# A row-half local operand, early work on the fourth quarter, and a doubled-step tail of the second scan chain in a one-core S5 / attention network

## The chip, the cores and the metric

The kernel runs on one core of a Trainium2 chip. The metric is the device time of one launch in microseconds (us), as the median of the runs given; one further execution was taken by the hardware profiler, and all rows below are from it. Engines are called as in the profile: PE (TensorE matmuls), PEld (TensorE weight loads), DVE (VectorE), ACT (ScalarE), POOL (GpSimd), SP (the DMA queue).

## What is computed

Two layers on one sequence of 256 tokens of width 2048. Layer 0 is an S5 state-space mixer, layer 1 a dilated windowed attention, each followed by a SwiGLU network. The change lies in the mixer alone:

```python
def s5_mixer(u, ...):                       # u: RMS-normed input, 128 groups of 16 channels
    lb  = exp((a_re + i a_im) * dt)         # 128 x 64 complex poles
    bb  = (lb - 1) / a * b                  # input map,  16 channels -> 64 states
    st[t] = lb * st[t-1] + bb @ u[t]        # a scan over the 256 tokens
    y[t]  = Re(c @ st[t]) + d * u[t]        # output map, 64 states -> 16 channels
    val, gate = split(gelu(y) @ w_glu)
    return val * sigmoid(gate)
```

## The kernel before

**Blocks of four tokens.** The 256 tokens are 64 blocks of four, so the scan has 63 steps by the fourth power of the poles. A block's output has two parts: `y_local`, from the four tokens of the block through a small dense operator `mt`, and `y_state`, from the state at the block's beginning through `fds`. The 128 groups are handled as four quarters (`qr` 0 to 3) of 32 groups; quarters 0 and 1 share the first scan chain (`sts[0]`), 2 and 3 the second (`sts[1]`). All helper calls of this function go through `InOrder`, so their instructions have line 59 in the profile, and stand on each engine in the order in which the code emits them.

**Order of the mixer.** Tables of powers and taps (DVE); `inject`: products that put each block's input into the states (PE, copied out by ACT); `build_m` for the four quarters (lines 458 to 478): the operator `mt`, then six small DMAs each that spread its bands; the scan (`scan`, lines 480 to 487: three DVE operations a step, one product by the table `fsc` and two additions, each needing the one before). `steps(n, sa, sb)` interleaves the two chains operation by operation. The first chain has a lead of 16 steps (`LEAD`), so when it is done (63 steps), 16 steps of the second remain; these are emitted in pieces between other DVE work (lines 650 to 670). While the scan runs, PE does `y_local` of quarters 0, 1, 2 and `y_state` for the first 32 blocks (`y_state(qr, yl[qr], range(8), 0, 32)`), and after the first chain's end `y_state` for blocks 32 to 63, `gelu` (ACT), `turn` (transposes on PE, high halves by ACT), `low` (low halves by DVE) and `feed` (the first block of the `w_glu` product: three matmuls of 512 columns for each part).

**`build_m` before.** Two groups' products stand side by side in a matmul with 128 rows and 64 columns. So that the two halves of the rows don't mix, `m_operand` (lines 450 to 456) writes a copy `cb` of `cp` with zeros in the other half, by ACT with a mask as scale: four ACT operations a quarter, queued on ACT behind the copies of the quarter before. Then 2 matmuls with the identity (256 columns, the skip term), 16 with `cb`, and two copies by ACT.

**PSUM.** `ps_ms` and `ps_tr` have two buffers each, `ps_mm` four. During the scan `ps_mm` holds its tables: `tbp` and `tbq` hold `fsc` and the scan's products `prs` until the second chain is done. Quarter 3's `y_local` is put into `ps_mm`, hence behind that chain (lines 679 and 680).

```python
        high(2, 0)
        feed(1, 1)
        rest(2, 0)
        y_state(2, yl[2], range(8), 32, 64)
        ...
        yl[3] = y_local(3, self.ps_mm, "mm")
        y_state(3, yl[3])
        turns(2)
```

From about 155 us on the program is a stream of weight chunks (1 MB each) with 512-column matmuls; nothing of the change touches it.

Of the kernel before, what the change touches and what calls it, by code (L numbers as in the profile page):

```python
# [20 lines left out]
P = 128  # L21
# [8 lines left out]
GI = 16  # L30
NS = 64
# [15 lines left out]

NW = 14
LEAD = 16


class InOrder:
# [9 lines left out]
class Net:  # L62
# [141 lines left out]
    def s5_glu(self):  # L204
        tc, nc, io = self.tc, self.nc, self.io
        late = tc.alloc_tile_pool(name="s5late", bufs=1)
        early = tc.alloc_tile_pool(name="s5early", bufs=1, side="right")
        V = nc.vector
        T, A, G, W = (InOrder(tc, e) for e in (nc.tensor, nc.scalar, nc.gpsimd, nc.vector))
# [35 lines left out]
        def tt(out, i, j, o, eng=None):  # L245
            (eng or V).tensor_tensor(out=out, in0=i, in1=j, op=o)
# [84 lines left out]
        pf = [form("pf1", lam)]  # L331
# [115 lines left out]
            for k in range(2):  # L447
                pair(cp[:, k, mo:mo + 16], cf[:, k, :, mo:mo + 16], ct[:, :, mo:mo + 16])

        def m_operand(qr, j4):  # L450
            m0 = 16 * qr + 8 * j4
            cb = early.tile([P, 2, 4, 2, 32], FP32, name="cb", tag="cb", bufs=2)
            src = cp[:, :, m0:m0 + 8].rearrange("p r (j x) o -> p r j (x o)", x=2)
            for y in range(2):
                A.activation(out=cb[:, :, :, y], in_=src, func=AF.Copy, scale=masks[:, y:y + 1])
            return cb

        def build_m(qr):
            cbs = [m_operand(qr, j4) for j4 in range(2)]
            ps = self.ps_ms.tile([P, 8, 2, 2, GI], FP32, name="ms")  # L460
            for xx in range(2):
                T.matmul(ps[:, :, :, xx], lhsT=self.ident,
                         rhs=dsm[:, 16 * qr:16 * qr + 16].rearrange("p (j y) o -> p j y o", y=2),
                         start=(xx == 0), stop=False, skip_group_check=True)
            for j in range(8):
                for ri in range(2):
                    T.matmul(ps[:, j], lhsT=gps[qr][:, ri, 2 * j:2 * j + 2].rearrange("p x s i -> p (x s i)"),
                             rhs=cbs[j // 4][:, ri, j % 4].rearrange("p y c -> p (y c)"),
                             start=False, stop=(ri == 1), skip_group_check=True)
            mo = 16 * qr  # L470
            for xx in range(2):
                r = slice(64 * xx, 64 * xx + 64)
                A.copy(out=mt[r, 3, mo:mo + 16].rearrange("p (j y) o -> p j y o", y=2), in_=ps[r, :, :, xx])
            for t in range(3):
                n = 16 * (t + 1)
                for xx in range(2):
                    nc.sync.dma_start(out=mt[64 * xx:64 * xx + n, t, mo:mo + 16],
                                      in_=mt[64 * xx + 64 - n:64 * xx + 64, 3, mo:mo + 16])

        def scan(h):  # L480
            st = sts[h]
            f, pr = fsc[h], prs[h]
            for c in range(63):
                hh, v = st[:, c], st[:, c + 1]
                yield lambda: tt(pr, f, hh.unsqueeze(1).broadcast_to([P, 2, 2, 32]), ALU.mult, W)
                yield lambda: tt(v, v, pr[:, :, 0], ALU.add, W)
                yield lambda: tt(v, v, pr[:, :, 1], ALU.add, W)

        def run(*its):
# [160 lines left out]
        for half in range(2):  # L650
            steps(3, sb)
            rest(0, half)
        steps(2, sb)
        pts = [turn(0, j4) for j4 in range(2)]
        y_state(1, yl[1], range(4, 8), 32, 64)
# [27 lines left out]
        feed(2, 0)  # L683
# [333 lines left out]
```

## Time and profile before

| quantity | us |
|---|---|
| median of 3 runs (2430.07 to 2431.36) | 2430.44 |
| the profiled execution's own time | 2428.69 |
| its span, first to last instruction | 2426.9 |
| PE busy in it | 2392.5 |
| DVE busy | 1323.8 |
| ACT busy | 1081.4 |

The profiled execution is 1.75 us below the median of the other runs; its span is 1.79 us below its own time. PE is busy for 99% of the span, but the profile counts a matmul that waits inside the engine as busy, and small fp32 matmuls are recorded as two matmuls and two weight loads each. A shape such as 64*128 in a row is rows*columns of the loaded weights; the shape behind it is what streams through.

### The profile page before, as it was taken

How to read it: one execution, taken by the hardware profiler on the slowest of the kernel's cores; microseconds unless marked ns; L12 is line 12 of the kernel's file. 1: busy time of each engine (PE TensorE's matmuls, PEld its weight loads, DVE VectorE, ACT ScalarE, POOL GpSimd, SP SyncE). 2: the span in 40 equal slices, each digit the busy share in tenths (PEclk: the TensorE clock that was granted, in tenths of full speed). 3: DMA queues.
4: the chain of work that ended last, by engine and by line, in shares of the span. 5: the costliest groups of instructions: out<-in, count | busy, mean ns of one | idle time of the engine just before them, and what ended most of it. 6: DMA issues, size and time to landing. Idle time of an engine off the chain costs nothing.

```text
span 2426.9 us, 29373 instructions
## 1 busy us (share of the span) xinstructions
PE 2392.5 (99%) x11856; PEld 1936.8 (80%) x11856; DVE 1323.8 (55%) x1974; ACT 1081.4 (45%) x1367; POOL 113.5 (5%) x113
## 2 busy tenths in 40 slices
PE   6899999999999999999999999999999999999999
PEld 5788888888888888888888888788888888888887
DVE  8955454454444454565446676765454444454454
ACT  7344444444334444554445555554444433344433
POOL 4800000000000000000000000100000000000000
PEclk9899999999999999999999999999999999999999
DMA  2345555555555555555554444445555555555554
GB/s 85 96 163 185 181 189 180 185 191 176 189 191 187 179 188 182 182 194 181 184 184 170 156 156 142 156 154 185 182 188 179 185 191 187 184 184 188 179 197 148
DMA packets 63033, 423.58 MB, mean 175 GB/s; under 512 B 8112, under 2 KB 9520, under 8 KB 12336
## 3 DMA queue, kind: packets, MB, share of 16 engines
q1 hardware_dynamic: 61744, 419.60, 50.7%
q8 instruction: 93, 1.52, 0.3%
q10 hardware_dynamic: 1152, 2.10, 0.2%
q14 instruction: 44, 0.36, 0.0%
HBM read 418.79 MB, written 2.10 MB: 173 GB/s over the span
## 4 chain that ended last, share of the span: by engine, by line
PE 97%; DVE 2%; ACT 1%; issue 0%; DMA 0%; POOL 0%; SPq 0%; DVEq 0%; POOLq 0%
PE mm L122 30%; PE mm L124 30%; PE mm L123 30%; PE ms L59 2%; PE tr L59 1%; PE ms L857 1%; PE tr L743 1%; PE mm L59 1%; PE tr L808 1%; DVE mm L59 0%; PE tr L857 0%; PE tr L185 0%; DVE gp L59 0%; DVE gpb L59 0%; PE ms L887 0%
## 5 line engine op out<-in xcount | busy, mean ns | idle before, releaser
L104 DVE TENSOR_TENSOR wlo<-raw,whi 128x1024 fp32r<-128x1024 f32 x776 | 948.5, 1224 | 1003.6 <-ACT whi L103 1002.1
L103 ACT CAST whi<-raw 128x1024 fp32r<-128x1024 f32 x776 | 813.0, 1048 | 1161.9 <-PE mm L124 1142.2
L122 PE MATMUL mm<-whi,actt 128*128 128x512 f32 x3104 | 1235.8, 398 | 1.4 <-ACT whi L103 1.4
L124 PE MATMUL mm<-whi,actt 128*128 128x512 f32 x3104 | 1229.6, 396 | 0.0
L123 PE MATMUL mm<-wlo,actt 128*128 128x512 f32 x3104 | 1229.3, 396 | 0.0
L124 PEld LDWEIGHTS mm<-whi,actt 128*128 128x128 f32 x3104 | 583.1, 188 | 139.2
L122 PEld LDWEIGHTS mm<-whi,actt 128*128 128x128 f32 x3104 | 583.1, 188 | 138.3 <-ACT whi L103 2.1
L123 PEld LDWEIGHTS mm<-wlo,actt 128*128 128x128 f32 x3104 | 583.2, 188 | 136.9 <-DVE wlo L104 0.4
L795 POOL TENSOR_TENSOR sc<-ssq,mhalf 128x8 f32<-128x8 f32 x16 | 32.1, 2005 | 475.0 <-DVE ssq L793 475.0
L174 POOL TENSOR_TENSOR r<-m,mhalf 128x1 f32<-128x1 f32 x6 | 3.2, 552 | 1053.1 <-DVE m L173 848.9
L59 DVE TENSOR_TENSOR actr<-actr,mm 128x64 f32<-128x64 f32 x252 | 46.7, 215 | 2.0
L729 ACT ACTIVATE sg<-mm,r 128x512 f32<-128x512 f32 x44 | 30.1, 690 | 21.3 <-PE mm L124 21.0
L59 DVE TENSOR_TENSOR mm<-mm,actr 128x128 f32<-128x128 f32 x126 | 37.0, 294 | 0.9
L866 ACT ACTIVATE s<-s,mx 128x384 f32<-128x384 f32 (+1 forms) x32 | 24.8, 774 | 25.1 <-DVE mx L864 25.1
L59 POOL TENSOR_TENSOR fpr<-pf,cp 128x512 f32<-128x512 f32 x32 | 34.9, 1092 | 0.0
L733 DVE SCALAR_TENSOR_TENSOR sg<-mm,r,sg 128x512 f32<-128x512 f32 x44 | 30.9, 742 | 0.0
L59 ACT COPY actr<-ms 128x252 f32<-128x252 f32 (+1 forms) x40 | 19.9, 580 | 22.5 <-PE ms L59 21.4
L791 ACT ACTIVATE sq<-mm 128x512 f32<-128x512 f32 x32 | 19.0, 594 | 23.5 <-PE mm L124 23.5
L871 DVE SCALAR_TENSOR_TENSOR p<-s,z,p 128x128 f32<-128x128 f32 (+1 forms) x64 | 26.3, 411 | 3.8 <-ACT p L869 3.6
L747 DVE TENSOR_TENSOR actt<-tr,actt 128x512 fp32r<-128x512 f32 x44 | 28.2, 681 | 0.0
L746 ACT CAST actt<-tr 128x512 fp32r<-128x512 f32 x44 | 23.7, 590 | 10.1 <-PE tr L743 10.1
L743 PEld LDWEIGHTS tr<-ident,sg 128*128 128x128 f32 x176 | 19.4, 140 | 9.2 <-DVE sg L733 9.2
(180 smaller groups left out, 946.8 us busy)
## 6 DMA issues: line engine op xcount, KB each, us to landing
raw<-w_gu SPq DMA_DIRECT2D x176, 1024.0 KB, 4.8
raw<-w_down SPq DMA_DIRECT2D x88, 1024.0 KB, 4.8
raw<-w_q SPq DMA_DIRECT2D x48, 1024.0 KB, 4.8
raw<-w_glu SPq DMA_DIRECT2D x32, 1024.0 KB, 4.8
raw<-w_kv SPq DMA_DIRECT2D x32, 1024.0 KB, 4.7
raw<-w_o SPq DMA_DIRECT2D x16, 1024.0 KB, 4.7
actr<-x_c SPq DMA_DIRECT2D x2, 1024.0 KB, 6.4
xr<-x_t SPq DMA_DIRECT2D x8, 256.0 KB, 5.8
```

Source lines behind the costliest of these rows:

```text
L59: return lambda *a, **k: self.tc.keep_in_program_order(call(*a, **k))
L103: (scalar or self.nc.scalar).copy(out=hi, in_=r)
L104: (vector or self.nc.vector).tensor_tensor(out=lo, in0=r, in1=hi.bitcast(FP32), op=ALU.subtract)
L122: matmul(ps[th], lhsT=a[:, 0, ts], rhs=hi, start=(k == 0), stop=False)
L123: matmul(ps[th], lhsT=a[:, 0, ts], rhs=lo, start=False, stop=False)
L124: matmul(ps[th], lhsT=a[:, 1, ts], rhs=hi, start=False, stop=(k == n - 1))
L729: nc.scalar.activation(out=s, in_=ps[th], func=AF.Silu, scale=rs[th])
L733: nc.vector.scalar_tensor_tensor(out=sg[th], in0=ps[th], scalar=rs[th], in1=sg[th], op0=ALU.mult, op1=ALU.mult)
L743: nc.tensor.transpose(out=pt[:, k, th * P:(th + 1) * P], in_=sg[th][:, c:c + P], identity=self.ident)
L747: nc.vector.tensor_tensor(out=ht[:, k0:k0 + 2, 1], in0=pt, in1=ht[:, k0:k0 + 2, 0].bitcast(FP32), op=ALU.subtract)
L795: nc.gpsimd.tensor_tensor(out=sc, in0=ssq, in1=self.mhalf.rearrange("p (a b) -> p a b", a=2), op=ALU.pow)
L871: nc.vector.scalar_tensor_tensor(out=pr, in0=sc[:, g], scalar=z, in1=pr, op0=ALU.mult, op1=ALU.add)
```

## The change

Three edits in the mixer, all before about 155 us.

**1. Row-half local operand.** `m_operand`, its masks and `cb` go. `build_m` now takes two PSUM tiles a quarter, one for each half of the rows: quarters 0 and 2 from `ps_ms`, 1 and 3 from `ps_tr`. The identity term is 4 matmuls of 128 columns instead of 2 of 256; the products are 32 matmuls of 64 rows and 32 columns, alternating between the two halves, instead of 16 of 128 rows and 64 columns; ACT copies four times 64x128 instead of twice 64x256.

**2. Second chain's tail.** `sb` ends after 47 steps (`LAST`). The squared table `f8` (eight tokens) is made by six DVE operations (`square`), interleaved with the first chain's solo steps. `tail`: four more single steps, interleaved with 18 operations (`lead_in`) that add each odd injection, times the table, to the next one for the last 12 blocks; then six units (`doubles`), each giving two blocks from one state: one product by `f8`, one by `fsc`, four additions.

**3. Quarter 3 ahead.** `y_local(3)` goes to `ps_ms` and, with `y_state(3)` for blocks 0 to 31, stands directly behind `feed(1, 1)`; blocks 32 to 63 follow after `gelu(yl[2])`. `turn` of quarters 2 and 3 takes `ps_mm` instead of `ps_ms`. The pieces of `sb` between `rest(0, 0)` and `rest(0, 1)` are four steps' worth of operations instead of three.

```diff
-        def m_operand(qr, j4):
-            ...
-                A.activation(out=cb[:, :, :, y], in_=src, func=AF.Copy, scale=masks[:, y:y + 1])
         def build_m(qr):
-            cbs = [m_operand(qr, j4) for j4 in range(2)]
-            ps = self.ps_ms.tile([P, 8, 2, 2, GI], FP32, name="ms")
-            ...
+            pool, nm = ((self.ps_ms, "ms"), (self.ps_tr, "tr"))[qr % 2]
+            ps = [pool.tile([P, 8, 2, GI], FP32, name=nm) for _ in range(2)]
             ...
             for j in range(8):
                 for ri in range(2):
-                    T.matmul(ps[:, j], lhsT=gps[qr][:, ri, 2 * j:2 * j + 2]...,
-                             rhs=cbs[j // 4][:, ri, j % 4]...)
+                    for y in range(2):
+                        r = slice(64 * y, 64 * y + 64)
+                        T.matmul(ps[y][:, j], lhsT=gps[qr][r, ri, 2 * j:2 * j + 2]...,
+                                 rhs=cp[r, ri, mo + 2 * j:mo + 2 * j + 2]...)
@@
-            for c in range(63):
+            for c in range(63 if h == 0 else LAST):
@@
+        def lead_in(c0):
+            for c in range(c0, 63, 4):
+                for k in range(2):
+                    yield lambda: tt(w4[k], f, st[:, c + 1 + 2 * k]..., ALU.mult, W)
+                for r in range(2):
+                    for k in range(2):
+                        v = st[:, c + 2 + 2 * k]
+                        yield lambda: tt(v, v, w4[k][:, :, r], ALU.add, W)
+        def doubles(c0):
+            for c in range(c0, 63, 2):
+                hh, v, w = (st[:, c + k] for k in range(3))
+                yield lambda: tt(pr8, f8, b, ALU.mult, W)
+                yield lambda: tt(prs[1], f, b, ALU.mult, W)
+                for r in range(2):
+                    yield lambda: tt(w, w, pr8[:, :, r], ALU.add, W)
+                    yield lambda: tt(v, v, prs[1][:, :, r], ALU.add, W)
@@
-        steps(LEAD - 6, sa)
+        run(itertools.islice(sa, 3 * (LEAD - 6)), square())
@@
+        sb = tail()
@@ def turn
-            pt = self.ps_ms.tile([P, 4, 2, NS], FP32, name="ms")
+            pt = (self.ps_ms.tile(..., name="ms") if qr < 2 else self.ps_mm.tile(..., name="mm"))
@@
         feed(1, 1)
+        yl[3] = y_local(3, self.ps_ms, "ms")
+        y_state(3, yl[3], range(8), 0, 32)
         rest(2, 0)
         y_state(2, yl[2], range(8), 32, 64)
         ...
         gms[2] = gelu(yl[2])
-        yl[3] = y_local(3, self.ps_mm, "mm")
-        y_state(3, yl[3])
+        y_state(3, yl[3], range(8), 32, 64)
         turns(2)
```

How the instructions now stand, at the places that matter. On PE, the four quarters of `build_m` (`cb` masked operand, `cp` plain operand, `gp_228` to `gp_231` the weights of quarters 0 to 3, `dsm` the skip term), before:

```order
L59 MATMUL ms<-dsm,ident 128x16x16 x2
L59 MATMUL ms<-cb,gp_228 128x64 x16
L59 MATMUL ms<-dsm,ident 128x16x16 x2
L59 MATMUL ms<-cb,gp_229 128x64 x16
L59 MATMUL ms<-dsm,ident 128x16x16 x2
L59 MATMUL ms<-cb,gp_230 128x64 x16
L59 MATMUL ms<-dsm,ident 128x16x16 x2
L59 MATMUL ms<-cb,gp_231 128x64 x16
```

and now:

```order
L60 MATMUL ms<-dsm,ident 128x8x16 x4
L60 MATMUL ms<-cp,gp_228 128x32 x32
L60 MATMUL tr<-dsm,ident 128x8x16 x4
L60 MATMUL tr<-cp,gp_229 128x32 x32
L60 MATMUL ms<-dsm,ident 128x8x16 x4
L60 MATMUL ms<-cp,gp_230 128x32 x32
L60 MATMUL tr<-dsm,ident 128x8x16 x4
L60 MATMUL tr<-cp,gp_231 128x32 x32
```

Twice as many matmuls of half the rows and half the columns, and the odd quarters write the other pool. On PE, from the last `feed` of the second chunk to the transposes of quarter 2 (`mm<-actr`, `ms<-actr`: `y_local` 64x64 and `y_state`, 32x64 for half of the blocks), before:

```order
L59 MATMUL tr<-whi,actt 128x512
L59 MATMUL mm<-actr 32x64 x64
L59 MATMUL mm<-actr 64x64 x96
L59 MATMUL ms<-ident,gm 128x128 x8
L59 MATMUL tr<-whi,actt 128x512
```

and now:

```order
L60 MATMUL tr<-whi,actt 128x512
L60 MATMUL ms<-actr 64x64 x32
L60 MATMUL ms<-actr 32x64 x64
L60 MATMUL mm<-actr 32x64 x64
L60 MATMUL ms<-actr 32x64 x64
L60 MATMUL mm<-ident,gm 128x128 x8
L60 MATMUL tr<-whi,actt 128x512
```

`y_local(3)` and half of `y_state(3)` moved ahead of quarter 2's second half, and `y_state(3)` is 128 matmuls of 32 instead of 64 of 64. On SP, the last six band copies (`actr<-actr`, quarter 3) and the first weight chunks, before:

```order
L477 DMA actr<-actr 48x256 x2
L96 DMA raw<-w_glu 128x2048
L477 DMA actr<-actr 16x256 x2
L477 DMA actr<-actr 32x256 x2
L477 DMA actr<-actr 48x256 x2
L96 DMA raw<-w_glu 128x2048 x2
L699 DMA xr<-x_t 128x512 x8
```

and now:

```order
L475 DMA actr<-actr 48x256 x2
L475 DMA actr<-actr 16x256 x2
L475 DMA actr<-actr 32x256 x2
L475 DMA actr<-actr 48x256 x2
L97 DMA raw<-w_glu 128x2048 x3
L752 DMA xr<-x_t 128x512 x8
```

The first chunk of `w_glu` stands behind those six copies instead of ahead of them.

## Rows read from the trace of the kernel before

**Rows 1.** The page: span; busy time, share and instructions of each engine; the shares of the chain that ended last by engine.

```profile
span 2426.9 us, 29373 instructions
...
PE 2392.5 (99%) x11856; PEld 1936.8 (80%) x11856; DVE 1323.8 (55%) x1974; ACT 1081.4 (45%) x1367; POOL 113.5 (5%) x113
...
PE 97%; DVE 2%; ACT 1%; issue 0%; DMA 0%; POOL 0%; SPq 0%; DVEq 0%; POOLq 0%
```

**Rows 2.** The chain that ended last, in order of time, 50 to 158 us: start, length, engine and tile ("issue": the engine waits for nothing that the profile shows).

```profile
61.42 0.69 ACT cb L59 x2
62.16 3.80 PE ms L59 x32
...
73.29 13.86 PE ms L59 x68
...
87.99 3.47 PE ms L59 x60
...
97.22 3.24 issue
...
103.23 5.78 PE mm L59 x172
...
110.91 0.83 issue
...
129.46 9.47 PE mm L59 x302
```

**Rows 3.** Busy time by stretch: from:to, length, busy us of PE, PEld, DVE, ACT, POOL, then the granted clock of TensorE (1.00 is 2.4 GHz, 0.50 is 1.2 GHz), DMA share and GB/s.

```profile
62.00:74.00 12.00, 10.11 (x78) 9.21 (x79) 12.00 (x79) 5.74 (x15) 11.53 (x14) 1.00 0.08 21
74.00:76.00 2.00, 2.00 (x19) 2.00 (x18) 2.00 (x14) 0.04 (x1) 1.92 (x3) 0.91 0.22 61
76.00:92.00 16.00, 15.56 (x127) 14.39 (x127) 16.00 (x106) 4.66 (x10) 15.29 (x19) 0.50 0.28 91
...
100.00:106.00 6.00, 5.54 (x145) 5.37 (x145) 5.86 (x37) 0.00 (x0) 5.76 (x7) 0.50 0.03 5
```

**Rows 4.** PE in order of time, the four quarters of `build_m`: start, length, instructions; in brackets the idle time before and what ended it.

```profile
60.47 1.10 PE L59 MATMUL ms<-dsm,ident 128*128 128x256 f32 x4
62.16 3.79 PE L59 MATMUL ms<-cb,gp 128*128 128x64 f32 x32 [0.59 <-ACT cb L59]
65.78 1.08 PE L59 MATMUL ms<-dsm,ident 128*128 128x256 f32 x4
67.73 3.79 PE L59 MATMUL ms<-cb,gp 128*128 128x64 f32 x32 [0.87 <-ACT cb L59]
...
73.29 4.97 PE L59 MATMUL ms<-cb,gp 128*128 128x64 f32 x32 [0.86 <-ACT cb L59]
...
80.05 7.09 PE L59 MATMUL ms<-cb,gp 128*128 128x64 f32 x32
```

**Rows 5.** PE in order of time, 14 to 53 us: the transposes of the second half's input, whose weights have 64 rows and 128 columns.

```profile
38.33 1.21 PE L59 MATMUL tr<-ident,actr 64*128 64x64 f32 x16
39.37 1.16 PE L59 MATMUL ms<-ident,actr 64*128 64x64 f32 x16
```

**Rows 6.** Weight loads by shape, 37 to 40 us and 50 to 60 us: count, busy us, mean ns of one, idle before.

```profile
L59 PEld LDWEIGHTS tr<-ident,actr 64*128 64x128 f32 x16 | 1.1, 139 | 0.2 <-issue 0.2
...
L59 PEld LDWEIGHTS tr<-ident,gp 128*128 128x128 f32 x16 | 1.7, 140 | 2.9 <-issue 2.6 <-DVE gp L59 0.3
```

**Rows 7.** Matmuls by shape, 129.3 to 132 us (first row, `y_state(2)`) and 132 to 139 us (`y_state(3)` and `y_local(3)`): count, busy us, mean ns.

```profile
L59 PE MATMUL mm<-actr 64*32 64x64 f32 x128 | 2.6, 235 | 0.0
...
L59 PE MATMUL mm<-actr 64*64 64x64 f32 x128 | 4.9, 305 | 0.0
L59 PE MATMUL mm<-actr 128*64 128x64 f32 x64 | 2.2, 225 | 0.0
```

**Rows 8.** DVE in order of time around the end of the first chain (two chains up to 105.3 us, the second alone from there) and at the end of the second; `wlo` is `rest`.

```profile
104.07 0.29 DVE L59 TENSOR_TENSOR mm<-mm,actr 128x128 f32<-128x128 f32 x1
...
104.53 0.29 DVE L59 TENSOR_TENSOR mm<-mm,actr 128x128 f32<-128x128 f32 x1
...
105.37 0.30 DVE L59 TENSOR_TENSOR mm<-mm,actr 128x128 f32<-128x128 f32 x1
...
106.21 0.30 DVE L59 TENSOR_TENSOR mm<-mm,actr 128x128 f32<-128x128 f32 x1
...
107.78 1.32 DVE L59 TENSOR_TENSOR wlo<-raw,whi 128x1024 fp32r<-128x1024 f32 x1
...
128.40 0.47 DVE L59 TENSOR_TENSOR actr<-actr,mm 128x64 f32<-128x64 f32 x2
```

**Rows 9.** SP's issues and ACT, in order of time: the first weight chunk, the last six band copies, and the first cast that reads that chunk.

```profile
87.17 0.33 SPq L96 DMA_DIRECT2D raw<-w_glu  x1
87.60 3.69 SPq L477 DMA_DIRECT2D actr<-actr  x6
...
92.31 2.02 ACT L59 CAST whi<-raw 128x1024 fp32r<-128x1024 f32 x2 [2.86 <-DVE mm L59]
```

**Rows 10.** PE in order of time, from `turn(2)` on.

```profile
138.86 1.09 PE L59 MATMUL ms<-ident,gm 128*128 128x128 f32 x8
140.21 0.50 PE L59 MATMUL tr<-whi,actt 128*128 128x512 f32 x1 [0.26 <-ACT actt L59]
...
141.30 0.73 PE L59 MATMUL tr<-whi,actt 128*128 128x512 f32 x2 [0.36 <-DVE actt L59]
```

More of the change, by code (lines that the diff above doesn't have):

```diff
@@ L49 @@
 LEAD = 16
+LAST = 63 - LEAD
 class InOrder:
@@ L448, in build_c, with build_m @@
                 pair(cp[:, k, mo:mo + 16], cf[:, k, :, mo:mo + 16], ct[:, :, mo:mo + 16])
-        def m_operand(qr, j4):
-            m0 = 16 * qr + 8 * j4
-            cb = early.tile([P, 2, 4, 2, 32], FP32, name="cb", tag="cb", bufs=2)
-            src = cp[:, :, m0:m0 + 8].rearrange("p r (j x) o -> p r j (x o)", x=2)
+        def build_m(qr):
+            pool, nm = ((self.ps_ms, "ms"), (self.ps_tr, "tr"))[qr % 2]
+            ps = [pool.tile([P, 8, 2, GI], FP32, name=nm) for _ in range(2)]
+            mo = 16 * qr
@@ L454, in m_operand @@
             for y in range(2):
-                A.activation(out=cb[:, :, :, y], in_=src, func=AF.Copy, scale=masks[:, y:y + 1])
-            return cb
-        def build_m(qr):
-            cbs = [m_operand(qr, j4) for j4 in range(2)]
-            ps = self.ps_ms.tile([P, 8, 2, 2, GI], FP32, name="ms")
[L461 to L464, printed above, removed]
+                for xx in range(2):
+                    T.matmul(ps[y][:, :, xx], lhsT=self.ident,
+                             rhs=dsm[:, mo:mo + 16].rearrange("p (j y) o -> p j y o", y=2)[:, :, y],
+                             start=(xx == 0), stop=False, skip_group_check=True)
@@ L465, in build_m @@
             for j in range(8):
                 for ri in range(2):
[L467 to L470, printed above, removed]
+                    for y in range(2):
+                        r = slice(64 * y, 64 * y + 64)
+                        T.matmul(ps[y][:, j], lhsT=gps[qr][r, ri, 2 * j:2 * j + 2].rearrange("p x s i -> p (x s i)"),
+                                 rhs=cp[r, ri, mo + 2 * j:mo + 2 * j + 2].rearrange("p x o -> p (x o)"),
+                                 start=False, stop=(ri == 1), skip_group_check=True)
@@ L471, in build_m @@
             for xx in range(2):
                 r = slice(64 * xx, 64 * xx + 64)
-                A.copy(out=mt[r, 3, mo:mo + 16].rearrange("p (j y) o -> p j y o", y=2), in_=ps[r, :, :, xx])
+                for y in range(2):
+                    A.copy(out=mt[r, 3, mo:mo + 16].rearrange("p (j y) o -> p j y o", y=2)[:, :, y],
+                           in_=ps[y][r, :, xx])
             for t in range(3):
@@ L487, in scan, with square @@
                 yield lambda: tt(v, v, pr[:, :, 1], ALU.add, W)
+        f8 = half(tbq[:, 256:384])
+        pr8 = half(tbp[:, 0:128])
+        w4 = [tbp[:, 256 + 128 * k:384 + 128 * k].rearrange("p (k r m) -> p k r m", k=2, r=2) for k in range(2)]
+        z8 = late.tile([P, 2, 32], FP32, name="z8")
+        def square():
+            z = pw[3][:, :, 32:64]
+            yield lambda: tt(pr8s, pf[3][:, :, :, 32:64], z.unsqueeze(1).broadcast_to([P, 2, 2, 32]), ALU.mult, W)
+            yield lambda: tt(z8, pr8s[:, :, 0], pr8s[:, :, 1], ALU.add, W)
+            yield lambda: W.tensor_copy(out=f8[:, 0, 0], in_=z8[:, 0])
+            yield lambda: W.tensor_copy(out=f8[:, 1, 1], in_=z8[:, 0])
+            yield lambda: W.tensor_copy(out=f8[:, 1, 0], in_=z8[:, 1])
+            yield lambda: W.tensor_scalar(out=f8[:, 0, 1], in0=z8[:, 1], scalar1=-1.0, scalar2=None, op0=ALU.mult)
@@ new lines, in s5_glu @@
+        pr8s = late.tile([P, 2, 2, 32], FP32, name="pr8s")
+        def lead_in(c0):
+            st, f = sts[1], fsc[1]
+            for c in range(c0, 63, 4):
+                for k in range(2):
+                    yield lambda: tt(w4[k], f, st[:, c + 1 + 2 * k].unsqueeze(1).broadcast_to([P, 2, 2, 32]),
+                                     ALU.mult, W)
+                for r in range(2):
+                    for k in range(2):
+                        v = st[:, c + 2 + 2 * k]
+                        yield lambda: tt(v, v, w4[k][:, :, r], ALU.add, W)
@@ new lines, in doubles @@
+        def doubles(c0):
+            st, f = sts[1], fsc[1]
+            for c in range(c0, 63, 2):
+                hh, v, w = (st[:, c + k] for k in range(3))
+                b = hh.unsqueeze(1).broadcast_to([P, 2, 2, 32])
+                yield lambda: tt(pr8, f8, b, ALU.mult, W)
[3 more added lines that the diff above has]
+                    yield lambda: tt(v, v, prs[1][:, :, r], ALU.add, W)
@@ new lines, in tail @@
+        def tail():
+            extra = lead_in(LAST + 4)
+            st, f, pr = sts[1], fsc[1], prs[1]
+            for c in range(LAST, LAST + 4):
+                hh, v = st[:, c], st[:, c + 1]
+                yield lambda: tt(pr, f, hh.unsqueeze(1).broadcast_to([P, 2, 2, 32]), ALU.mult, W)
+                yield from itertools.islice(extra, 2)
+                yield lambda: tt(v, v, pr[:, :, 0], ALU.add, W)
+                yield from itertools.islice(extra, 1)
+                yield lambda: tt(v, v, pr[:, :, 1], ALU.add, W)
+                yield from itertools.islice(extra, 2)
+            yield from extra
+            yield from doubles(LAST + 4)
@@ L623, in turn @@
                 lhs.extend(gtile[qr // 2][:, k] for k in range(8))
-            pt = self.ps_ms.tile([P, 4, 2, NS], FP32, name="ms")
+            pt = (self.ps_ms.tile([P, 4, 2, NS], FP32, name="ms") if qr < 2 else
+                  self.ps_mm.tile([P, 4, 2, NS], FP32, name="mm"))
             for t in range(4):
@@ L649, in s5_glu @@
         y_state(1, yl[1], range(4), 32, 64)
-        for half in range(2):
-            steps(3, sb)
-            rest(0, half)
+        for c in range(2):
+            steps(4, sb)
+            rest(0, c)
         steps(2, sb)
```

## The prediction

> **What bounds the kernel now.** The page first: PE is 97% of the chain that ended last [rows 1]. The chain in order of time then shows where a change of the mixer can count [rows 2]: from 62.16 us to the steady stream of weights it runs through PE nearly all the time. It passes the four quarters of `build_m` (62.16 to 87.15), `y_local(0)` at 87.99, a stop of 3.24 us at 97.22, `y_local(2)` from 103.23, the half of `y_state` that follows the first chain, a stop of 0.83 at 110.91, and 9.47 us of quarters 2 and 3 at 129.46. The scan on DVE isn't on it there: the first chain's last operation ends at 104.74 + 0.60 = 105.3 [rows 8], while PE comes to the work that needs it at 103.23 + 5.78 = 109.0 [rows 2]. So PE is 3.7 us behind the scan at this meeting point. That is the most that a faster `build_m` can give there, and each microsecond beyond it belongs to DVE.
>
> The stretches show the clock of that time [rows 3]: full (2.4 GHz) to 74 us, half (1.2 GHz) from 76 to 92, half again from 100 to 106. Before the first fall PE had stopped 0.59, 0.87 and 0.86 us for ACT's `cb`, once a quarter [rows 4]; before the second it had the stop of 3.24 us [rows 2].
>
> **The change, part by part.**
>
> *Local operand.* A quarter now takes 67.73 - 62.16 = 5.57 us at the full clock [rows 4]: 16 matmuls, recorded as 32, in 65.78 - 62.16 = 3.62 us, 113 ns a record; the identity terms, about 1.0 us; and the stop for `cb`. The stop goes, since `cp` is read as it is, and the new tiles come from two pools in turn, so that copies of one quarter run beside products of the next. The identity terms stay at 4 x 256 = 8 x 128 recorded columns, so about 1.0 us. The 32 new matmuls are 64 records with weights of 64 rows and 128 columns. The trace has this load only in transposes, 16 of them from 38.33 to 39.37, 65 ns each [rows 5]. From below, records of 64*64, four tiles in turn, took 4.9 us for 128, 38 ns [rows 7]; from above, the 113 ns of the present records, should a load of half the rows cost as much as a full one and nothing run beside it. I take 60 ns, nearest to the 65 of the same load and a little under it, since half as many columns stream and the two halves alternate: 64 x 0.060 = 3.8 us, a quarter 4.8.
>
> The first products can start at about 61.9: the second PSUM tile is free when the last copy before `cb`, at 61.42 [rows 2], is done, and two identity terms follow. At the full clock the quarters end at 65.7, 70.5, 75.3 and 80.1. I take it that the clock falls about where it fell; the last quarter then costs 2 x 4.8 = 9.6 and ends at 84.9. `y_local(0)` need not wait for the copies of quarter 3 any more (these are now in the other pool), so it starts there and not at 87.99: **3.1 us earlier**. PE then meets the scan at 109.0 - 3.1 = 105.9, still after 105.3, so all of it counts.
>
> The trace bears on this edit in one row more: a weight load of 64 rows took 139 ns and one of 128 rows 140, both for 128 columns [rows 6]. The Trainium skill, "TensorE: Matmul & The Clock Gate", section on LDWEIGHTS, says that a load's time goes by its columns and not by the rows; by that rule, which these rows bear out, twice as many loads are twice the loading, and the sum would be that of the third rival below.
>
> *The scan's tail.* Now 16 steps of the second chain alone, at 106.21 - 105.37 = 0.84 us each, 13.5 us. With two chains a step costs 104.53 - 104.07 = 0.46 for three operations, 0.155 us each, because one chain's operation fills the other's wait [rows 8]. The tail has 4 x 3 + 18 + 6 x 6 = 66 operations, always two independent ones in turn: 66 x 0.155 = 10.2 us. DVE gains 3.3 us. What of it shows: at present the chain ends at 128.40 + 0.47 = 128.9 [rows 8] and PE asks for it at 129.46 [rows 2], so it is hidden by 0.6 us. With PE 3.1 us earlier it would be late by 2.5; the gain of 3.3, and the 2.2 + 2.6 = 4.8 us of quarter 3 that now stand ahead of the need [rows 7], cover that. So this edit and the third are worth nothing by themselves but keep the first one's gain. Should the tail run at the old 0.28 us an operation, it would take 18.5 us and end 5.0 later; quarter 3's work covers 4.8 of these, and the early PE makes the rest visible. The six operations of `square` lie between solo operations of the first chain: from nothing to 6 x 0.155 = 0.9 us; they stand ahead of the meeting point at 105.3, where PE has 0.6 left. I take 0.2, hidden.
>
> *Quarter 3 ahead.* `y_state(3)` in two halves is two times the 2.6 us of 128 records of 64*32 instead of 4.9 for 64*64 [rows 7]: **+0.3 us** on PE; from below 0, from above +0.6 if a change between tile shapes stops PE. `y_local(3)` costs its 2.2 us in either place. `turn(2)` and its waits of 0.26 and 0.36 us for ACT and DVE [rows 10] follow as before.
>
> *Queues.* SP now issues the first weight chunk after the last six copies, whose issue took 3.69 us [rows 9]. With `build_m` 3 us earlier the chunk comes about 1 us later than the 87.17 of now. Its first cast ran at 92.31, and DVE needs it at 107.78 [rows 8]: 13 us of cover. If that were gone, at most the 3.7 us would show at `rest(0, 0)`. ACT loses 16 mask operations and gains 8 copies, on an engine that waits for PE there. POOL's work is the same.
>
> Sum: -3.1 + 0.3 = **-2.8 us**. Against the profiled execution's own 2428.7 that is 2425.9; it lies 1.75 under the median of the runs (the table above has both), so against that median: 2430.4 - 2.8 = **2427.6 us**.
>
> **The rivals.**
>
> *The scan bounds it (faster, a little more).* If PE, which no longer stops for `cb`, keeps its full clock through `build_m`, the last quarter ends at 80.1, and PE waits for the scan at 105.3 instead. Gain 3.7, perhaps also the stop of 0.83 us, whose cause would have time to pass: 3.7 + 0.8 - 0.3 = 4.2, 2426.2 us. For it: each of those stops goes. Against: a PE that waits for DVE loses its clock, as it did after 97.22 [rows 2, 3], and gives part back.
>
> *The clock is lost early (slower).* The new records stream a quarter of the elements each, in half of the rows, and PE may be too little busy to keep 2.4 GHz from the first quarter on. Three quarters at 9.6 us after 65.7 end at 94.5, 6.5 us after the 87.99 of now: 2430.4 + 6.5 + 0.3 = 2437.2. It decides as soon as `y_local(0)` starts after 88.0. For it: at half clock two quarters of `build_m` did not bring the clock back between 76 and 92 [rows 3, 4]. Against: at the full clock the present records, almost as sparse, kept it from 62 to 74 us.
>
> *A half load costs a full one (slower).* 113 ns a record: 64 x 0.113 = 7.2, a quarter 8.2 us. Quarter 1 ends at 69.1, and by 75.7, where the clock falls, 6.6 of the remaining 24.6 are done; 18.0 at half speed end at 111.7. That is 23.7 late: 2454. For it: rows 6. Against: 65 ns a record in rows 5, with the same load. [...]
>
> *Nothing shows.* The stop of 3.24 us moves or grows with the start of the weight chunks and takes the gain: 2430.4, give or take 0.5.
>
> **How the numbers follow.** My forecast 0.50, scan bounds 0.19, clock lost early 0.17, full loads 0.07, nothing shows 0.07. The range goes from the scan's bound, 2426.2, a little lower for stops that vanish, to the early clock: 2425.6 to 2437.4; beyond it lie the full loads and a little of the others. A measurement of this kernel can tell about 0.2%, 4.9 us. My forecast and the scan's bound lie within it, bar 0.05 for more stops vanishing than I count; the early clock lies outside for 0.15 of its 0.17 (it may fall a quarter later), the full loads entirely. So faster 0.05, within 0.73, slower 0.22.
>
> **What would show it.** Right: no idle time with ACT `cb` before the products; a quarter of about 4.8 us at the full clock; `y_local(0)` at about 85; PE on blocks 32 to 63 at about 106, just after the first chain; DVE's tail in about 10 us of its own time, done before `y_state(2)` asks; quarters 2 and 3 on PE in about 9.8 us. Wrong: records of 64*128 at over 80 ns; a granted clock of 0.50 before 72 us; PE idle on DVE for more than 1 us at the meeting point; `y_state(2)` waiting for DVE.

## The result, and the profile after

| kernel | median, us | executions |
|---|---|---|
| before, same chip | 2430.4 | 9 |
| changed | 2436.8 | 9 |
| ratio, 95% interval | 1.0029 | 1.0020 to 1.0037 |

Slower by 0.3%, where 2427.6 was forecast. The changed kernel's profiled execution took 2437.79 us, its span is 2436.0. Two executions of over 3300 us, one of before and one of e9, are left out in all that follows.

The chain that ended last, in order of time (answers to [rows 2]): start, length, engine and tile.

```profile
62.79 4.40 PE ms L60 x68
67.19 8.50 PE tr L60 x72
75.69 8.97 PE ms L60 x72
84.67 8.97 PE tr L60 x72
93.64 3.61 PE ms L60 x64
...
102.52 3.02 issue
...
115.87 1.31 issue
...
135.37 4.24 PE ms L60 x176
...
141.06 0.73 issue
...
144.01 1.51 issue
...
155.51 0.73 PE mm L123 x2
```

The stretches; the granted clock is the third number from the end, as in [rows 3]:

```profile
62.00:74.00 12.00, 11.66 (x130) 11.09 (x131) 11.84 (x74) 1.58 (x6) 11.53 (x14) 0.74 0.07 18
74.00:76.00 2.00, 2.00 (x18) 1.94 (x18) 2.00 (x15) 0.28 (x2) 1.87 (x3) 0.50 0.02 4
76.00:92.00 16.00, 16.00 (x132) 15.49 (x131) 16.00 (x105) 1.41 (x7) 15.34 (x18) 0.50 0.10 26
```

PE in order of time, the products of the first two quarters (against [rows 4]):

```profile
63.43 3.76 PE L60 MATMUL ms<-cp,gp 64*128 64x32 f32 x64
67.12 1.60 PE L60 MATMUL tr<-dsm,ident 128*128 128x128 f32 x8
68.65 7.04 PE L60 MATMUL tr<-cp,gp 64*128 64x32 f32 x64
```

What the reader is to see: the stops for `cb` are gone, and a record takes (67.12 - 63.43) / 64 = 58 ns at 2.4 GHz. But the second quarter takes 7.04 us, 110 ns a record: the clock is at 1.2 GHz from the second quarter on, while before it held to 74 us. So `y_local(0)` starts at 93.6 instead of 87.99 (+5.6), and all that follows is late by as much. Quarters 2 and 3 then take from 135.37 to 146.59, 11.2 us instead of 9.47 [rows 2] (+1.7), with two stops marked issue. The weight stream starts at 155.51; that of before started 147.84 us into its span, 7.7 earlier. The spans differ by 9.1; the other 1.4 lie in the attention, where the clock was 0.91 between 1580 and 1600 us and before 1.00. The medians differ by 6.4, since the two profiled executions lie on opposite sides of theirs.

DVE in order of time, the two solo steps with the operations of `square` among them:

```profile
52.63 0.30 DVE L60 TENSOR_TENSOR mm<-mm,actr 128x128 f32<-128x128 f32 x1
52.84 0.35 DVE L60 TENSOR_TENSOR pr8s<-pf,pw 128x128 f32<-128x128 f32 x1
53.11 0.21 DVE L60 TENSOR_TENSOR actr<-actr,mm 128x64 f32<-128x64 f32 x1
53.24 0.94 DVE L60 TENSOR_TENSOR z<-pr8s 128x64 f32<-128x64 f32 x1
...
56.12 0.30 DVE L60 TENSOR_TENSOR mm<-mm,actr 128x128 f32<-128x128 f32 x1
```

From 52.63 to 56.12 is 3.49 us, against 2 x 0.84 for plain steps: the first chain ends 1.8 us later. In this execution that is hidden, because PE comes later still. The same engine in the tail (`doubles`):

```profile
131.46 0.62 DVE L60 TENSOR_TENSOR mm<-mm,actr 128x128 f32<-128x128 f32 x2
132.12 0.61 DVE L60 TENSOR_TENSOR actr<-actr,mm 128x64 f32<-128x64 f32 x4
132.77 0.63 DVE L60 TENSOR_TENSOR mm<-mm,actr 128x128 f32<-128x128 f32 x2
```

Six operations in 1.31 us, 0.22 each, where I had taken 0.155.

### The profile page after: what moved, and what is told of

The parts are those of the page before. It is cut to its first block, busy times and chain, and to the rows that moved or that the text cites. A ratio compares the mean times of both kernels' runs of the same rounds, so it can differ in the third digit from the quotient of the medians.

```text
span 2436.0 us, 29938 instructions
## 1 busy us (share of the span) xinstructions
PE 2399.1 (98%) x12128; PEld 1942.5 (80%) x12128; DVE 1328.0 (55%) x1998; ACT 1075.6 (44%) x1359; POOL 112.5 (5%) x113
## 4 chain that ended last, share of the span: by engine, by line
PE 97%; DVE 2%; ACT 1%; issue 0%; DMA 0%; POOL 0%; SPq 0%; DVEq 0%; POOLq 0%
PE mm L123 30%; PE mm L125 30%; PE mm L124 30%; PE tr L60 2%; PE ms L60 1%; PE ms L910 1%; PE tr L796 1%; PE tr L861 1%; DVE mm L60 0%; PE tr L910 0%; PE tr L186 0%; DVE gp L60 0%; PE mm L60 0%; DVE gpb L60 0%; PE ms L940 0%
## 5 line engine op out<-in xcount | busy, mean ns | idle before, releaser
L796 PE MATMUL tr<-ident,sg 128*128 128x128 f32 x176 | 26.7, 274 | 0.0
```

What stands on the lines that cost most here:

```text
L796: nc.tensor.transpose(out=pt[:, k, th * P:(th + 1) * P], in_=sg[th][:, c:c + P], identity=self.ident)
```

## The experiments

Theory 1: the narrow products lose the clock in `build_m`. Rival, theory 2: more PE instructions cost stops. Every kernel was timed beside the kernel before, though not all on the same chip (medians of before there 2428.7 to 2429.9). Ratios are against it; between kernels timed on different chips they tell more than the times do.

### One edit at a time

**e1_local**, before with edit 1 alone:

```diff
-        def m_operand(qr, j4): ...
-        def build_m(qr): ...          # 16 products, 128 rows x 64 columns
+        def build_m(qr): ...          # 32 products, 64 rows x 32 columns
```

> The kernel before with the row-half local operand alone. Theory 1 (the half-row, 32-column products do not hold the 2.4 GHz clock; it falls in the first quarter and stays at 1.2 until y_local): granted clock 0.50 from about 68 us on, y_local(0) at 93 to 94 us instead of 87.99, time +5 to +6 us over the kernel before, about 2436. Theory 2 (the time goes into stops of instruction fetch, in the split y_state(3) above all): this edit brings its forecast gain or little, -3 to +1 us, 2427 to 2431. Theory 3 (the clock's fall in the changed kernel came from the preceding stage, by chance): clock falls at 74 to 76 us as before, -3 us, 2427.5.

2435.8 us, ratio 1.0027 (1.0015 to 1.0038); granted clock of all six executions 0.989 to 0.991, and `y_local(0)` at 92.7:

```profile
92.72 2.51 PE L59 MATMUL ms<-actr 128*64 128x64 f32 x42
```

Theory 1 as expected; 2 and 3 fall for this edit.

**e2_rest**, edits 2 and 3 alone:

```diff
-        def build_m(qr): ...          # of the change
+        def m_operand(qr, j4): ...
+        def build_m(qr): ...          # of before
-        z8 = late.tile(...)
+        z8 = gpb[1]...                # pr8s likewise in gpb[0]
```

> The changed kernel with the masked operand cb put back: the scan's tail and quarter 3 ahead alone (the temporaries of square lie in gpb here, since SBUF is full with cb). Theory 1: build_m as before, so y_local(0) at about 88 and the time within +0.3 of the kernel before if quarter 3 costs what I forecast. Theory 2: the 128 more records of y_state(3) bring the stops marked issue, 0.7 to 1.5 us each, and quarters 2 and 3 take 11.2 instead of 9.5 us: +1.5 to +2.2 us, about 2432. Both may hold; their sum, 5.6 + 1.7, would be 7.3 against the 7.7 us by which the weight stream starts later in the changed kernel's trace.

2434.5, ratio 1.0025 (1.0015 to 1.0034): more than either theory gave, so the two halves, +6.7 and +5.4, don't add up to the +6.4 of the whole. PE, in order of time:

```profile
106.92 3.66 PE L60 MATMUL ms<-fdx,actr 64*32 64x64 f32 x128 [2.40 <-DVE actr L60]
...
137.74 0.82 PE L60 MATMUL mm<-actr 64*32 64x64 f32 x32 [1.46 <-issue]
...
141.20 0.81 PE L60 MATMUL ms<-actr 64*32 64x64 f32 x32 [0.92 <-issue]
```

With the clock kept (1.00 to 96.8 us here) PE is early, and a second cost shows: it waits for a first chain that ends at 107. The later of PE and scan counts at the meeting point, so a late PE and a late scan hide each other.

### What loses the clock

**e8_r128n32** and **e9_r64n64** change one dimension of the product each. e8, from e3_ahead (below):

```diff
-                    T.matmul(ps[:, j], ..., rhs=cbs[j // 4][:, ri, j % 4]...)      # 64 columns
+                    for y in range(2):
+                        T.matmul(ps[:, j, y], ..., rhs=cbs[j // 4][:, ri, j % 4, y])
```

> e3_ahead (masked operand, no stops) with each product of 128 rows and 64 columns cut into two of 128 rows and 32 columns: as many matmuls as in the changed kernel, full rows. If the few columns or the number of matmuls lose the clock: 0.50 from the first or second quarter on as in e1_local, clock of the execution 0.990, y_local(0) at 93 or later, 2435 or more. If the half rows lose it: clock kept until past 85 us as in e3_ahead. The time then goes by the records: at 57 ns each y_local(0) at 79 and 2428; at 113 ns (a full load each) a quarter of 8.2 us, y_local(0) at about 95, 2434 to 2436 though the clock is kept.

e9, from e1_local:

```diff
-                        T.matmul(ps[y][:, j], ..., rhs=cp[r, ri, mo + 2*j:mo + 2*j + 2]...)
+                        k = min(j, 6)
+                        T.matmul(ps[y][:, k:k + 2], ..., rhs=cp[r, ri, mo + 2*k:mo + 2*k + 4]...)
```

> e1_local with products of 64 rows and 64 columns instead of 32: each also streams the neighbour's columns, so the local operand's values are changed. If the half rows lose the clock: as e1_local, 0.50 from about 67 us, 2435 to 2437. If the few columns lose it: clock at 1.00 past 74 us, y_local(0) at 81 to 85 (57 ns a record), 2428 to 2430. If both play a part, the clock falls one or two quarters later than in e1_local, 2431 to 2434.

e8: 2460.1, ratio 1.0132 (1.0118 to 1.0146). e9: 2429.1, ratio 0.9993 (0.9984 to 1.0002). Stretches of e8, then of e9, columns as above:

```profile
62.00:74.00 12.00, 12.00 (x66) 11.81 (x66) 12.00 (x79) 2.40 (x7) 11.53 (x14) 0.61 0.01 2
```

```profile
62.00:74.00 12.00, 12.00 (x188) 11.62 (x188) 12.00 (x78) 1.69 (x8) 11.53 (x14) 1.00 0.10 25
...
76.00:92.00 16.00, 13.76 (x469) 13.28 (x467) 16.00 (x105) 5.81 (x11) 15.29 (x19) 1.00 0.65 224
```

PE in order of time, products of e9, then of e8:

```profile
61.99 3.79 PE L59 MATMUL ms<-cp,gp 64*128 64x64 f32 x64
```

```profile
75.00 13.70 PE L59 MATMUL tr<-cb,gp 128*128 128x32 f32 x64
```

Half rows with 64 columns keep 1.00, full rows with 32 columns lose it: the narrow stream does it, not the half rows. And twice the columns cost no time (3.79 us against 3.76), since the weight loads fill it (PEld, the second busy time in e9's first row: 11.62 of 12.00 us). In e8, where successive loads share all rows, a record took 214 ns at 1.2 GHz, against 110 with alternating halves in the changed kernel. The Trainium skill, "TensorE: Matmul & The Clock Gate", section "Part 3: Packing small matmuls", says that a load overlaps a running matmul only in other rows; the two rows agree. They don't separate this from a load of half the rows being cheaper in itself: the loads of [rows 5], 65 ns a record, all go to the same 64 rows (`build_u` in the code, one `h` for all of them).

**e10_pad**, the changed kernel with each product streaming its 32 columns twice:

```diff
-                                 rhs=cp[r, ri, ...].rearrange("p x o -> p (x o)"),
+                                 rhs=cp[r, ri, ...].rearrange("p x o -> p (x o)")
+                                 .unsqueeze(1).broadcast_to([64, 2, 32]),   # second copy into unused PSUM
```

> The changed kernel with one difference: each row-half product streams its 32 columns twice (64 columns, the second copy into unused PSUM). In e9_r64n64 this width cost no time (64 records in 3.79 us) and the clock stayed at 1.00 to 95 us. Theory 1 (too few columns streamed in build_m lose the clock): clock at 1.00 through build_m, y_local(0) at about 80 to 82 instead of 93.57; PE then waits for the scan, which square delays to about 106.9, and quarter 3's stops remain: as e2_rest, 2432.5 to 2434.5, clock of the execution 0.994 to 0.996, 2 to 4 us under the changed kernel's 2436.8. If the clock was not what cost the changed kernel: 2436 to 2438 again.

2433.7, ratio 1.0017 (1.0009 to 1.0026), 3.1 under the changed kernel, clock 1.00 through `build_m`, `y_local(0)` at 79.8, and PE then waits 7.13 us for the scan. Two stretches, then PE in order of time:

```profile
62.00:74.00 12.00, 12.00 (x192) 11.62 (x190) 11.86 (x75) 1.69 (x8) 11.45 (x14) 1.00 0.09 25
76.00:92.00 16.00, 13.43 (x466) 12.94 (x464) 16.00 (x106) 5.44 (x9) 15.37 (x18) 1.00 0.60 211
```

```profile
79.77 2.08 PE L60 MATMUL ms<-actr 128*64 128x64 f32 x64
...
106.38 3.37 PE L60 MATMUL ms<-fdx,actr 64*32 64x64 f32 x128 [7.13 <-DVE actr L60]
```

As expected: the clock's loss is shown, and so is that something else holds the kernel at 2433.7.

**e4_dense**, a smaller dose of dense work:

```diff
-                T.matmul(ps[y][:, :, xx], lhsT=self.ident, ...)      # 4, at the start
+                T.matmul(ps[y][:, :, xx], lhsT=ident2, ...)          # 4 at the start, 4 among the products
```

> The changed kernel with the skip term (identity matmuls of 128 columns over all 128 rows) added in two halves, four at the quarter's start as now and four spread among the row-half products, with half the identity as weights: 8 more records a quarter, about 1.1 us of PE time at the full clock. Theory 1: the products' sparseness loses the clock, so dense work among them holds it longer: clock at 1.00 beyond 68 us; if held through all four quarters (5.9 us each from 61.9), y_local(0) at about 85.5, 8 us earlier than in the changed kernel, time 2429 to 2431. If this dose is too small to hold it, or density is not the cause: three quarters at 11.8 us, y_local(0) at about 103, 2443 to 2446.

2452.1, ratio 1.0098 (1.0084 to 1.0111). The clock was 0.50 from 66.2 us on, in the first quarter, and `y_local(0)` came at 108.8: the dose bought nothing, and its price was paid at half speed. My expectation was low by 6 us, and that dense matmuls among the products hold the clock is not shown by this run.

### The scan and `square`

**e3_ahead**, before with `cb` of the next quarter built ahead:

```diff
-            cbs = [m_operand(qr, j4) for j4 in range(2)]
-            ps = self.ps_ms.tile(...)
+            cbs = ahead.pop(qr) if qr in ahead else [m_operand(qr, j4) for j4 in range(2)]
+            ps = (self.ps_ms, self.ps_tr)[qr % 2].tile(...)
...
+            if qr < 3:
+                ahead[qr + 1] = [m_operand(qr + 1, j4) for j4 in range(2)]   # before the copies
```

> The kernel before, with cb of the next quarter built on ACT ahead of this quarter's copies, and odd quarters of build_m in ps_tr; the products stay 128 rows by 64 columns. The three stops for cb (0.59, 0.87, 0.86) and the 0.84 us ahead of y_local(0) go. Theory 1 (what costs the clock is the half rows and 32 columns, not that the stops go): clock falls no earlier than 74 us, y_local(0) at about 85, -3 us, 2427.5. If the stops are what costs the kernel before its clock: full clock through build_m, y_local(0) at 80 to 81, and the scan bounds it: -3.7 to -4.5, 2426 to 2426.7. If a denser build_m gains nothing, because the stop marked issue ahead of y_state takes it up: within 0.5 of the kernel before.

2427.9, ratio 0.9997 (0.9988 to 1.0006): clock kept through `build_m`, `y_local(0)` at 78.9, nine us earlier than before's [rows 2], and no gain that can be told. PE waits for the scan:

```profile
104.78 3.66 PE L59 MATMUL ms<-fdx,actr 64*32 64x64 f32 x128 [4.45 <-DVE actr L59]
```

**e15_square**, e3_ahead with `square` among the solo steps, result unused:

```diff
-        steps(LEAD - 6, sa)
+        run(itertools.islice(sa, 3 * (LEAD - 6)), square())
```

> e3_ahead with the six operations of square between the first chain's solo steps, its result unused; nothing else. In e3_ahead PE waits 4.45 us for DVE at the meeting point, so a delay of the first chain counts in full. Theory: two steps in 3.5 us instead of 1.68, meeting point at 106.7 instead of 104.78, +1.8 to +2.1 us, 2429.8 to 2430. If the chip takes it up later (PE catches up, a stop shrinks): within 0.7 of e3_ahead, 2427.9 to 2428.6.

2430.4, ratio 1.0000 (0.9992 to 1.0009), 2.5 above e3_ahead:

```profile
106.69 3.66 PE L59 MATMUL ms<-fdx,actr 64*32 64x64 f32 x128 [6.78 <-DVE actr L59]
```

The meeting point moved by 1.9 us, as expected. The times were taken on two chips: by the ratios e15_square is 0.7 us dearer than e3_ahead, with intervals that overlap, so `square`'s delay is shown at the meeting point and its price in the whole time is not measured closely.

### The split of quarter 3

**e14_split**, before with one line in two:

```diff
-        y_state(3, yl[3])
+        y_state(3, yl[3], range(8), 0, 32)
+        y_state(3, yl[3], range(8), 32, 64)
```

> The kernel before with y_state(3) in two halves at its old place: 128 matmuls of 64*32 instead of 64 of 64*64, nothing else. By the records' own durations +0.3 us. Theory 2 (instructions arrive at a limited rate: in the traces 16 KB of PE instructions every 3.6 to 3.9 us, and a stop marked issue after each 256): quarters 2 and 3 in 11 to 12 us instead of 9.5, +1.5 to +2.3 us, 2431 to 2432. If the instructions are there in time at this place: +0.3, 2430.

2432.2 against 2429.3, ratio 1.0008 (1.0000 to 1.0017). **e17_slack** puts cheap work in front:

```diff
         feed(1, 1)
+        pad = self.ps_ms.tile([P, 4, P], FP32, name="ms")
+        for k in range(8):
+            T.transpose(out=pad[:, k % 4], in_=self.ident, identity=self.ident)
```

> e14_split with eight transposes of the identity (16 PE records, about 2.2 us by the 136 ns of the transposes of turn, results unused) put between feed(1, 1) and quarter 2's second half. If the stops of 1.21 and 1.71 us come because instructions arrive too slowly for matmuls of 20 ns, the transposes give them time: the stops shrink by about 2 us, the time stays within 0.7 of e14_split's 2432.2. If the stops belong to the split matmuls themselves, they stay, and the time is 2 us more, 2434 to 2434.6.

PE in order of time, e14, then e17:

```profile
105.03 3.63 PE L59 MATMUL ms<-fdx,actr 64*32 64x64 f32 x128 [0.68 <-DVE actr L59]
...
128.59 6.80 PE L59 MATMUL mm<-actr 64*32 64x64 f32 x288
136.60 2.29 PE L59 MATMUL mm<-actr 64*32 64x64 f32 x128 [1.21 <-issue]
140.61 0.81 PE L59 MATMUL mm<-actr 64*32 64x64 f32 x32 [1.71 <-issue]
141.35 1.10 PE L59 MATMUL ms<-ident,gm 128*128 128x128 f32 x8
```

```profile
137.80 2.32 PE L59 MATMUL mm<-actr 64*32 64x64 f32 x128 [0.86 <-issue]
141.53 0.96 PE L59 MATMUL mm<-actr 64*32 64x64 f32 x40 [1.41 <-issue]
```

In e14 quarters 2 and 3 took 12.8 us (128.59 to 141.35) instead of 9.47 [rows 2], more than the 11 to 12 that I expected. In e17 the transposes were 8 records and 1.0 us, not 16 and 2.2. The stops shrank from 2.92 to 2.27 us, so 0.65 of the 1.0 was taken up; the time, 2432.7 (ratio 1.0021, 1.0012 to 1.0030), is too near to tell. In both, and in the changed kernel (141.79 to 145.52), 3.7 to 4.0 us lie between the restarts, for 128 records whose own work is 2.3. That PE's instructions arrive at this rate is the likeliest reading, not a shown one. The split's cost is shown in PE's time; in the whole time (e14's ratio) it is at the edge of the noise.

**e5_unsplit**, e2_rest without the split:

```diff
-        y_state(3, yl[3], range(8), 0, 32)
...
-        y_state(3, yl[3], range(8), 32, 64)
+        y_state(3, yl[3])
```

> Tail and quarter 3 ahead without the local operand, as in e2_rest, but with y_state(3) in one piece (64 matmuls of 64*64 instead of 128 of 64*32), behind gelu(yl[2]); y_local(3) still ahead. Theory 2 (the split's 128 more PE records bring stops of instruction fetch): quarters 2 and 3 on PE in 9.5 us again instead of 11.8 in e2_rest, at most one stop marked issue; about 2 us under e2_rest, 2432 to 2433. If the stops come from the place and not from the number of instructions, no change against e2_rest, 2434.5.

2433.3, ratio 1.0016 (1.0007 to 1.0025), 1.2 under e2_rest (by the ratios 2.2), with executions from 2428 to 2437; quarters 2 and 3 still took 11.0 us in the profiled one, with one stop of 1.48. By the times that is half of what I expected, by the ratios all of it, and the intervals overlap. In e18 (below) the same instructions of quarters 2 and 3 ran without a stop, so the stop doesn't come from their number alone.

### The whole account

**e7_sqtail** and **e11_padtail** move `square` to the tail's start, in e2_rest and in before with e10's operand and the tail:

```diff
-        run(itertools.islice(sa, 3 * (LEAD - 6)), square())
+        steps(LEAD - 6, sa)
-            extra = lead_in(LAST + 4)
+            extra = itertools.chain(square(), lead_in(LAST + 4))
```

> As e2_rest, but the six operations of square stand at the start of the second chain's tail instead of between the solo steps of the first chain. In the trace of e2_rest the two steps with square took 52.90 to 56.41, 3.5 us, against 1.68 for two plain ones, and PE waited 2.40 us for DVE at the meeting point. Theory: square delays the first chain by 1.8 to 2.1 us, and with a build_m at the full clock all of it counts: meeting point at about 105 instead of 106.9, 2432.5 to 2433. Rival: PE is late there anyhow in most executions, or a later stop takes it up: within 0.7 of e2_rest.

> The kernel before with the doubled-column row-half operand and the doubled-step tail, but square at the tail's start (its temporaries in their own tiles) and quarter 3 where it was. By the three costs found (clock, square on the first chain, split of y_state(3)) all are gone: y_local(0) at 80 to 82, meeting point at 105, no wait for DVE at y_state(2): 2427 to 2428.5, 8 to 10 us under the changed kernel and within 2 of the kernel before, which the scan bounds. If a cost is missing from the account, it shows as over 2430.

2442.6, ratio 1.0059 (1.0045 to 1.0073), and 2436.0, ratio 1.0024 (1.0016 to 1.0033): both missed by far. The waits of e11 by engine and tile, 80 to 118 us (total, times, longest):

```profile
ACT whi L60 <- DMA raw<-w_glu: 19.7, 1, 19.7
```

The second weight chunk (the expectation of e16 calls it the third) takes memory of `pw`, which `square` now read late: SP's issue of it waited 20.3 us for `pr8s`, the operation that reads `pw`. In e7 ACT's wait was 31.6 us; in e16 it is 3.15. **e16_tailpf** and **e18_repairs** read `pf` instead; e18 is the changed kernel with e10's columns, this `square` and e5's `y_state(3)`:

```diff
-            z = pw[3][:, :, 32:64]
+            z = pf[3][:, :, 0, 32:64]
```

> e11_padtail with square reading the table pf instead of pw, whose memory the third weight chunk takes. If that was what held e11_padtail (ACT waited 19.66 us for the chunk and gelu came 4.3 us late): the chunk issues at about 86 us, no wait of 4.32 us for gm, 2427 to 2429, 7 to 9 us under it. If square at the tail's start is dear in itself: y_state(2) still waits over 1 us for DVE, 2430 to 2432.

> The changed kernel with the three costs undone: columns streamed twice in build_m, square at the tail's start (reading pf), y_state(3) in one piece behind gelu(yl[2]). If clock (about 3 us, since the scan bounds what is left), square (2) and split (2) are the account: 7 to 8 us under the changed kernel, 2428.5 to 2430.5, within 0.1% of the kernel before. If quarter 3's y_local ahead, or the transposes in the other pool, cost something of their own: 2431 to 2433, as e5_unsplit.

e16: 2433.5, ratio 1.0011 (1.0002 to 1.0020): its second case, and dearer than I put it. PE, in order of time:

```profile
131.82 10.64 PE L60 MATMUL mm<-actr 64*32 64x64 f32 x320 [2.69 <-DVE actr L60]
```

With `square` in it the tail, from 105.2 to 131.8 with the other DVE work that stands in it, ends no sooner than the 16 plain steps of before, which ended at 128.9 [rows 8]. e18: 2428.9, ratio 0.9993 (0.9984 to 1.0002), 7.9 under the changed kernel and as expected. PE, in order of time:

```profile
81.60 2.09 PE L60 MATMUL ms<-actr 128*64 128x64 f32 x64
...
105.70 3.45 PE L60 MATMUL ms<-fdx,actr 64*32 64x64 f32 x128 [5.42 <-DVE actr L60]
...
133.96 2.62 PE L60 MATMUL mm<-actr 64*32 64x64 f32 x128 [0.43 <-DVE actr L60]
```

The three costs, undone together, give the whole loss back; what `square` and the split each cost in the changed kernel was not separated. Nothing is gained beyond, because the scan bounds it.

**e12_warm** asks what PE's wait for the scan costs, on before with e10's operand:

```diff
         y_state(2, yl[2], range(8), 0, 32)
+        for k in range(6):
+            T.matmul(yl[2][k % 2][:, 0:4], lhsT=self.ident, rhs=zeros, start=False, ...)
```

> The kernel before with the row-half operand streamed twice, and six matmuls of 256 columns by a tile of zeros (3.3 us at the full clock) where PE waits for the first chain. In e9_r64n64 PE waited 4.38 us there, and the clock was 0.50 from 94.9 to 108.6, so that y_state(0) for blocks 32 to 63 took 3.66 us instead of 2.6. If PE's idling is what loses that clock and matmuls with zeros count as work: 1.00 at 105 to 109, -1.0 to -2.0 us against e9_r64n64, 2427 to 2428. If zeros don't hold it: 2429 as e9_r64n64; if PE comes too late for them in many executions: 2430 or more.

```profile
99.89 2.86 PE L59 MATMUL mm<-zeros,ident 128*128 128x256 f32 x12
105.11 2.63 PE L59 MATMUL ms<-fdx,actr 64*32 64x64 f32 x128 [2.36 <-DVE actr L59]
...
115.33 1.22 PE L59 MATMUL tr<-whi,actt 128*128 128x512 f32 x2 [1.89 <-DVE actt L59]
```

PE in order of time: the clock is kept, and the 128 records of `y_state(0)` take 2.63 us, in e9 3.66. Yet 2429.9, ratio 0.9996 (0.9987 to 1.0006): the first `feed` then waits 1.89 us for DVE's `low`, in e9 1.02, and goes on at 115.33, in e9 at 115.15. DVE bounds this stretch too. No version beat the kernel before by more than the measurement tells. What a `build_m` that keeps its clock did change is the scatter: of 128 executions of before in all, 25 took over 2432 us, the longest 2436.2; of the 54 of e3, e9, e12, e15 and e18, none did (e10, e11 and e16 keep the clock too, but have costs of their own). That the 25 had lost the clock earlier than the profiled execution fits (granted clock 0.990 to 0.992 where it is listed, the changed kernel's 0.990 to 0.991), but none of them was profiled.

## Why the prediction was wrong

DVE in order of time, the end of the first chain in before, from which the prediction has its 105.3 us:

```profile
104.74 0.60 DVE L59 TENSOR_TENSOR actr<-actr,mm 128x64 f32<-128x64 f32 x3
```

- **What bounds it: right for one execution.** PE was 3.7 us behind the scan [rows 2, 8], but that execution had lost its clock at 75 us. In the six profiled executions with this `build_m` the clock fell at 75 us (before, e17), 81 (e14, e5), 97 (e2) and 102 (e7). In e14's PE waited 0.68 us for DVE. Of 27 executions of before beside e18, those with a granted clock of 0.995 to 0.997 took 2427.5 to 2429.5 us, those of 0.990 and 0.991 took 2431.4 to 2436.2. So in many there was little or nothing to gain from a faster `build_m`, and much to lose; I had read one draw as the kernel. The stop at 97.22, which I gave against the first rival as a wait for DVE, is marked issue [rows 2].
- **The step that failed:** "I take it that the clock falls about where it fell". It fell in the second quarter. The forecast put `y_local(0)` at 84.9, 3.1 us early; it came at 93.6, 5.6 us late. The second rival had mechanism and place, and 0.17 of the chances. That its time, 2437.2, lies so near the 2436.8 is in part luck: its 6.5 us for `y_local(0)` were 5.6, its 0.3 for quarter 3 was 1.7. My argument against it, that the present records were almost as sparse and kept the clock, overlooked that these lost it themselves in four of the six, inside `build_m`, as the falls at 75 and 81 us show. What in a narrow stream loses the clock stays open.
- **A record's price: right.** 60 ns taken, 58 measured; a quarter of 4.8 us, measured in e10 (61.63 to 66.44). The rival of a full load for half the rows falls. The 139 and 140 ns of [rows 6], its support, are the length of one load; the loads of 139 ns followed each other every 65 ns [rows 5].
- **The tail: hidden, as forecast, but mis-sized.** 0.155 us an operation taken, 0.22 measured; by the code a unit's two products need the last unit's additions, which is the likely reason. `square` was taken at 0.2 and bounded by 0.9; it is 1.8 (3.49 - 1.68), hidden in the changed kernel, bare as soon as PE is early (e15, e10).
- **Quarter 3 ahead: mis-sized.** +0.3 taken, +0.6 the upper bound, +1.7 measured; I priced the matmuls' own time and no stop for issue, though before had the stop of 0.83 us marked issue in the same kind of matmuls [rows 2].
- **Queues: right that nothing shows**, though the first chunk was issued at 97.92, not 1 but 11 us later than [rows 9].

## What to carry to other kernels

Before pricing a faster PE stage, look at several executions' granted clock: a profile that happens to hold a slow clock offers a gain that most executions don't have. Where weight loads bound small matmuls, fewer columns save no time and may lose the clock; streaming the same columns twice cost nothing here. Operations tucked between a dependent chain's steps are not free, even if the engine looks idle.

## What the runs showed of the hardware

- Behind matmuls with a tile of zeros TensorE was still at 2.4 GHz after a wait of 2.36 us (e12, granted clock 1.00 from 99 to 108 us); without them, after 4.38 us (e9), it was at 1.2. The zeros and the shorter wait are not separated.
- The addition `z<-pr8s`, 64 elements from SBUF, took 0.94 us, one with an operand in PSUM 0.21 just before it. POOL then worked from 53.00 to 54.11, and the addition ended at 54.18; in e15 it was 53.07 to 54.18, and 54.25. The Trainium skill, "SBUF — State Buffer", section "SBUF: two separate sides", says that a DVE operation with two SBUF inputs and a POOL operation that reads SBUF exclude each other; that fits, and no run here separates it. POOL in order of time, the changed kernel:

```profile
53.00 1.11 POOL L60 TENSOR_TENSOR fpr<-pf,cp 128x512 f32<-128x512 f32 x1
54.18 0.73 POOL L60 TENSOR_TENSOR fdx<-fpr 128x256 f32<-128x256 f32 x1
```
